# Retention heads of a decoder step: the samples' states weighted by q on ScalarE and VectorE, and the last block of scores in three fp32r passes

## Chip, cores and metric

One core of one Trainium2 chip runs the whole program. The metric is the device time of one execution in microseconds; the kernel before takes 2317.14 us in the median of 3 runs (2315.48 to 2318.4).

## The reference, cut to what matters

One layer of a hybrid decoder works on 256 prompt rows and 8 sample rows at once. The part that the change touches is retention: 8 heads, 256 channels of q and k, 512 of v per head. For the prompt, in chunks of 128 rows:

```python
scores = jnp.einsum('bhld,bhmd->bhlm', q, k) * decay[None]
q_dec = q * jnp.exp((idx[None, :] + 1.0) * log_g[:, None])[None, :, :, None]
o = jnp.einsum('bhlm,bhmv->bhlv', scores, v) + jnp.einsum('bhld,bhdv->bhlv', q_dec, S)
k_dec = k * jnp.exp((L - 1.0 - idx[None, :]) * log_g[:, None])[None, :, :, None]
S_new = jnp.exp(L * log_g)[None, :, None, None] * S + jnp.einsum('bhmd,bhmv->bhdv', k_dec, v)
```

For each of the 8 samples there is one new row and a state S of 256 x 512 per head, read from memory: S becomes g S + k v, is written back, and the output row is q S (512 numbers per sample and head). Then follow a group norm over each head's 512 channels, a gate, and projections. All of it is fp32.

## The kernel before, in words

Activations stand transposed: channels on the 128 partitions, 264 columns (256 prompt rows, 8 samples). Every large product is a stream over weight chunks of 512 x 256 (`gemm`, `project`): SyncE loads a chunk, ScalarE rounds it to fp32r (`wh_...`, line 199), VectorE takes the remainder (`wl_...`, line 200), and TensorE makes 24 matmuls of 128x128 by 264 columns, three fp32r passes for each tile (`gemm_part`, lines 213 to 215). Three buffers each hold `wh` and `wl`, six the raw chunks.

The stretch around the change is the loop over the 8 heads. While head h does its retention, TensorE works on the input projections of head h + 1 (`acc_in`), on the output projection of head h - 1 (`acc_pa`) and on the modulation (`mp`, with 32-column weights in four column groups of the array). `spread` lays the 18 steps of `retention` between these chunks, and a scheduler in the framework then sets the order on each engine; engines take their instructions strictly in that order, so the order is fixed before the run.

The steps of one head that matter:

- `sample_rows`, `scores`, `values`, `keys` prepare: the samples' v rows (`vsr`), the decayed scores, the transposed v blocks in two halves m = 0 and 1 (`vh`, `vl`), k times its decay.
- `sample(b)`, eight times: GpSimd's queue loads the state tile `S` (128 x 2 x 512), VectorE copies v's row b to all partitions (`vb`, line 620), ScalarE multiplies `S` by the head's g (line 621), VectorE adds k v in two instructions (line 623), GpSimd's queue stores `S`.
- `sample_q(half)`, twice: q S on TensorE. For four samples and both halves d of the 256 channels there is a matmul of 32 weight columns (`z`, a q column set among zeros, copied by GpSimd at line 546) and 512 moving columns (line 634), each sample in its own column group, all into one tile `qp`. `S` has to stay until then.
- `sample_out`: `qp` holds the eight rows spread over the column groups; four fp32 matmuls with a 0/1 matrix of 8 columns (line 644, `osp`) gather and transpose them into `o`.
- `prompt_out(i)`: for each of the four blocks of 128 v channels, three fp32r matmuls over 256 columns for m = 0 (lines 597 to 599) and one plain fp32 matmul over 128 columns for m = 1 (line 600, from `vt` and `sct`).
- `prompt_state`, `centre`, `gate` (line 610 is the last product of `prompt_state`) end the head; their `yh`, `yl` feed `project` of the next head.

Of the kernel before, what the change touches and what calls it, by code (L numbers as in the profile page):

```python
# [20 lines left out]
F32 = mybir.dt.float32  # L21
F32R = mybir.dt.float32r
AF = mybir.ActivationFunctionType
ALU = mybir.AluOpType
# [27 lines left out]
C_SELQ = C_SELM + 9  # L52
C_KD = C_SELQ + 8
# [7 lines left out]
def constants():  # L61
# [7 lines left out]
    for j in range(4):  # L69
        for i in range(9):  # L70
            c[32 * j + i, C_SELM + i] = 1.0
        c[32 * j + j, C_SELQ + j] = 1.0
        c[32 * j + 4 + j, C_SELQ + 4 + j] = 1.0
# [59 lines left out]
def build(ctx, tc, a):  # L133
# [365 lines left out]
    qz = []  # L499
    for i in range(2):  # L500
        z = hp.tile([P, 2, 2, 32], F32, tag=f"qz{i}", name=f"qz{i}")
        ve.memset(z, 0.0)
        qz.append(z)
# [25 lines left out]
    def retention(h):  # L529

        q, k, v, gr = raw_q[h], raw_k[h], raw_v[h], raw_gr[h]
        z = qz[h % 2]
        st = {}

        def sample_rows():
# [8 lines left out]
            for half in range(2):  # L544
                c = slice(4 * half, 4 * half + 4)
                gp.tensor_copy(out=z[:, half, :, c], in_=q[:, :, TP + 4 * half:TP + 4 * half + 4])

        def scores():
# [8 lines left out]
            st["sct"] = hp.tile([P, 384], F32, tag="sct", name=f"sct{h}")  # L557
            ve.tensor_tensor(out=st["sct"], in0=scp[:, :384], in1=dec, op=ALU.mult)
            st["scs"] = [hp.tile([P, 256], F32R, tag=f"sc{n}", name=f"sc{n}{h}") for n in ("hi", "lo")]
            split_act(st["sct"][:, 0:256], *st["scs"])  # L560

        def values(m):
# [6 lines left out]
            if m:  # L569
                st["vt"] = hp.tile([P, DV], F32, tag="vt", name=f"vt{h}")  # L570
                sc.copy(out=st["vt"], in_=vtp)
            split_act(st["vt"] if m else vtp, vh, vl)
# [15 lines left out]
        def prompt_out(i):  # L588
# [3 lines left out]
            (vh, vl), (sh, sl) = st["vs", 0], st["scs"]  # L592
            for j in range(2):
                vi = 2 * i + j
                c = slice(vi * P, (vi + 1) * P)
                out = op[:, j * 256:j * 256 + 256]
                te.matmul(out=out, lhsT=vh[:, c], rhs=sh, start=True, stop=False)
                te.matmul(out=out, lhsT=vh[:, c], rhs=sl, start=False, stop=False)
                te.matmul(out=out, lhsT=vl[:, c], rhs=sh, start=False, stop=False)
                te.matmul(out=out[:, P:], lhsT=st["vt"][:, c], rhs=st["sct"][:, 256:384], start=False, stop=True)  # L600
# [14 lines left out]
        def sample(b):  # L615

            s = hp.tile([P, 2, DV], F32, tag="S", name=f"S{h}_{b}", bufs=5)
# [8 lines left out]
            st["S", b] = s  # L626

        def sample_q(half):
# [3 lines left out]
            for d in range(2):  # L632
                for j in range(4):
# [334 lines left out]
```

## Time and profile before

| | |
|---|---|
| median of 3 runs | 2317.14 us (2315.48 to 2318.4) |
| the profiled execution's own time | 2321.42 us |
| its span, first to last instruction | 2319.7 us |
| PE busy in the span | 2288.5 us (99%) |
| VectorE (DVE) busy | 1457.3 us (63%) |
| ScalarE (ACT) busy | 1054.6 us (45%) |
| GpSimd (POOL) busy | 233.7 us (10%) |
| granted TensorE clock, mean | 0.997 |

The profile records each instruction of one execution with its start and its duration. Matmuls overlap in the array: one of 264 columns is recorded with 0.28 us, but the next starts 0.12 us later. So what a matmul costs is read here from start to start, not from its duration. A plain fp32 matmul is recorded as two instructions, an fp32r matmul or a transpose as one. PEld are the weight loads, which run beside the matmuls.

### The profile page before, as it was taken

What the parts mean: (1) busy time and instruction counts of PE and PEld (TensorE: products, weight loads), DVE (VectorE), ACT (ScalarE), POOL (GpSimd) and SP (SyncE); (2) the same over time, 40 slices, a digit from 0 to 9 for tenths busy, and PEclk for the clock granted to TensorE, in tenths of its full rate; (3) what the DMA queues carried; (4) which work ended last, traced back from release to release, by engine and by line L of the source; (5) the groups of instructions that cost most, each with busy time, mean ns of one, the idle gap of its engine ahead of it and who ended that gap; (6) DMA issues with size and microseconds to landing.
All of it is one profiled execution on the core that took longest, in us unless ns stands there. A gap on an engine that the chain in (4) does not pass through costs nothing. (4 is left out here: it accounts for less than half of the span.)

```text
span 2319.7 us, 44798 instructions
## 1 busy us (share of the span) xinstructions
PE 2288.5 (99%) x18496; PEld 2141.6 (92%) x18496; DVE 1457.3 (63%) x2078; ACT 1054.6 (45%) x1306; POOL 233.7 (10%) x404
## 2 busy tenths in 40 slices
PE   8999999999999999999999999999999999999997
PEld 6899998898998989898989999989999999999997
DVE  4676675676666666666665567576666666654444
ACT  4333354345454444454435454454444444444342
POOL 0000132021112020102010101111000000000000
PEclk9999999999999999999999999999999999999998
DMA  9788877897779696869687879856666665565663
GB/s 325 243 264 274 263 211 260 300 345 284 263 270 326 201 326 198 293 221 326 200 282 229 277 244 324 323 170 192 207 201 196 201 213 183 182 192 185 189 190 104
DMA packets 171581, 561.14 MB, mean 242 GB/s; under 512 B 18448, under 2 KB 32848, under 8 KB 171376
## 3 DMA queue, kind: packets, MB, share of 16 engines
q1 hardware_dynamic: 147376, 474.08, 62.8%
q0 software_dynamic: 23568, 83.73, 10.0%
q8 instruction: 145, 2.38, 0.4%
q10 hardware_dynamic: 432, 0.47, 0.1%
q14 instruction: 60, 0.49, 0.1%
HBM read 509.82 MB, written 48.38 MB: 241 GB/s over the span
## 5 line engine op out<-in xcount | busy, mean ns | idle before, releaser
L213 PE MATMUL acc_up<-h_hi,wh_up 128*128 128x264 f32 x1408 | 400.9, 285 | 1.6 <-ACT h_hi L204 1.6
L214 PE MATMUL acc_up<-h_lo,wh_up 128*128 128x264 f32 x1408 | 400.2, 284 | 0.6 <-DVE h_lo L205 0.6
L215 PE MATMUL acc_up<-h_hi,wl_up 128*128 128x264 f32 x1408 | 399.5, 284 | 0.0
L213 PE MATMUL acc_in<-h_hi,wh_in 128*128 128x264 f32 x1344 | 388.3, 289 | 0.0
L214 PE MATMUL acc_in<-h_lo,wh_in 128*128 128x264 f32 x1344 | 382.6, 285 | 0.0
L215 PE MATMUL acc_in<-h_hi,wl_in 128*128 128x264 f32 x1344 | 381.6, 284 | 0.0
L200 DVE TENSOR_TENSOR wl_up<-w_up,wh_up 128x1024 fp32r<-128x1024 f32 x176 | 215.9, 1227 | 179.7 <-ACT wh_up L199 179.5
L200 DVE TENSOR_TENSOR wl_in<-w_in,wh_in 128x1024 fp32r<-128x1024 f32 x168 | 205.0, 1222 | 158.3 <-ACT wh_in L199 142.4
L199 ACT CAST wh_in<-w_in 128x1024 fp32r<-128x1024 f32 x168 | 175.9, 1048 | 272.6 <-PE acc_in L214 162.3
L199 ACT CAST wh_up<-w_up 128x1024 fp32r<-128x1024 f32 x176 | 184.6, 1049 | 250.0 <-issue 142.8
L213 PEld LDWEIGHTS acc_up<-h_hi,wh_up 128*128 128x128 f32 x1408 | 265.4, 189 | 8.3 <-issue 5.9
L213 PEld LDWEIGHTS acc_in<-h_hi,wh_in 128*128 128x128 f32 x1344 | 252.9, 188 | 19.8 <-issue 14.3
L214 PEld LDWEIGHTS acc_up<-h_lo,wh_up 128*128 128x128 f32 x1408 | 265.7, 189 | 0.8 <-DVE h_lo L205 0.8
L215 PEld LDWEIGHTS acc_up<-h_hi,wl_up 128*128 128x128 f32 x1408 | 265.1, 188 | 0.0
L215 PEld LDWEIGHTS acc_in<-h_hi,wl_in 128*128 128x128 f32 x1344 | 252.5, 188 | 6.1 <-issue 5.0
L214 PEld LDWEIGHTS acc_in<-h_lo,wh_in 128*128 128x128 f32 x1344 | 253.0, 188 | 1.3 <-issue 0.8
L213 PE MATMUL acc_st<-h_hi,wh_st 128*128 128x264 f32 x704 | 203.7, 290 | 0.3 <-ACT ue L402 0.3
L215 PE MATMUL acc_st<-h_hi,wl_st 128*128 128x264 f32 x704 | 200.5, 286 | 2.2 <-DVE wl_st L200 2.2
L214 PE MATMUL acc_st<-h_lo,wh_st 128*128 128x264 f32 x704 | 199.9, 284 | 0.0
L214 PE MATMUL acc_dn<-f_lo,wh_dn 128*128 128x264 f32 x704 | 199.7, 284 | 0.0
L215 PE MATMUL acc_dn<-f_hi,wl_dn 128*128 128x264 f32 x704 | 199.6, 284 | 0.0
L213 PE MATMUL acc_dn<-f_hi,wh_dn 128*128 128x264 f32 x704 | 199.6, 284 | 0.0
(257 smaller groups left out, 5254.1 us busy)
## 6 DMA issues: line engine op xcount, KB each, us to landing
wm<-in_w_mod SPq DMA_DIRECT2D x176, 512.0 KB, 5.1
w_up<-in_w_up SPq DMA_DIRECT2D x176, 512.0 KB, 4.3
w_in<-in_w_in SPq DMA_DIRECT2D x168, 512.0 KB, 5.2
w_dn<-in_w_down SPq DMA_DIRECT2D x88, 512.0 KB, 3.7
S<-in_state_ret POOLq DMA_DIRECT2D x64, 512.0 KB, 7.8
out_rs<-S POOLq DMA_DIRECT2D x64, 512.0 KB, 5.0
w_pa<-in_w_proj_a SPq DMA_DIRECT2D x64, 512.0 KB, 4.4
w_st<-in_w_in SPq DMA_DIRECT2D x66, 384.0 KB, 4.2
```

Of the source, the lines that this page charges most:

```text
L199: sc.copy(out=hi, in_=w)
L200: ve.tensor_tensor(out=lo, in0=w, in1=hi.bitcast(F32), op=ALU.subtract)
L213: te.matmul(out=acc[:, b, :T], lhsT=hi[:, k, cols], rhs=xh[:, k0 + k, :], start=s, stop=False)
L214: te.matmul(out=acc[:, b, :T], lhsT=hi[:, k, cols], rhs=xl[:, k0 + k, :], start=False, stop=False)
L215: te.matmul(out=acc[:, b, :T], lhsT=lo[:, k, cols], rhs=xh[:, k0 + k, :], start=False, stop=e)
```

## The change

`sample(b)` now goes on after the update of `S`: ScalarE multiplies the first half of the state by q's column (`qt`, 128 x 512), and VectorE multiplies the second half by q's other column and adds it to `qt`. `S` is free after that and the store, and its buffers go from 5 to 4; `qt` has 4. `sample_q(half)` then has only to add up the 128 partitions: one matmul per sample with `pick`, whose 32 columns are ones in column 0 (first half) or 1 (second half) and zeros elsewhere. `sample_out` takes four transposes in place of the four selection matmuls, and VectorE's copy picks the eight rows out. The GpSimd copies into `z` are gone.

For m = 1 of `prompt_out` the plain fp32 matmul becomes three fp32r passes over 128 columns. The scores of all 384 columns are rounded and split, in place of 256, the copy `vt` is gone, and `dec` is overwritten in place of a tile `sct`.

```diff
@@ -49,8 +49,7 @@
 
 C_ID = 0
 C_SELM = C_ID + P
-C_SELQ = C_SELM + 9
-C_KD = C_SELQ + 8
+C_KD = C_SELM + 9
 C_CNT = C_KD + 16
 C_N = C_CNT + 64
 
@@ -69,8 +68,6 @@
     for j in range(4):
         for i in range(9):
             c[32 * j + i, C_SELM + i] = 1.0
-        c[32 * j + j, C_SELQ + j] = 1.0
-        c[32 * j + 4 + j, C_SELQ + 4 + j] = 1.0
     g = 1.0 - 2.0 ** (-5.0 - np.arange(H, dtype=np.float64))
     m = np.arange(TP, dtype=np.float64)
     for h in range(H):
@@ -496,11 +493,11 @@
     psum_phase("heads", True)
     rot = hp.tile([P, 2 * T], F32, tag="rot", name="rot")
     gp.dma_start(out=rot, in_=a["rot"])
-    qz = []
+
+    pick = hp.tile([P, 2, 32], F32, tag="pick", name="pick")
+    ve.memset(pick, 0.0)
     for i in range(2):
-        z = hp.tile([P, 2, 2, 32], F32, tag=f"qz{i}", name=f"qz{i}")
-        ve.memset(z, 0.0)
-        qz.append(z)
+        ve.memset(pick[:, i, i:i + 1], 1.0)
 
     def rotate(x0, x1, dst, scale, name):
         cos, sin = rot[:, 0:T], rot[:, T:2 * T]
@@ -529,7 +526,6 @@
     def retention(h):
 
         q, k, v, gr = raw_q[h], raw_k[h], raw_v[h], raw_gr[h]
-        z = qz[h % 2]
         st = {}
 
         def sample_rows():
@@ -541,9 +537,6 @@
                 te.transpose(vsp[:, i * P:(i + 1) * P], vsc[:, i].rearrange("p r b -> p (r b)"), ident)
             st["vsr"] = hp.tile([P, DV], F32, tag="vsr", name=f"vsr{h}")
             sc.copy(out=st["vsr"], in_=vsp)
-            for half in range(2):
-                c = slice(4 * half, 4 * half + 4)
-                gp.tensor_copy(out=z[:, half, :, c], in_=q[:, :, TP + 4 * half:TP + 4 * half + 4])
 
         def scores():
 
@@ -554,10 +547,9 @@
                 for d in range(2):
                     te.matmul(out=scp[:, c0:c0 + n], lhsT=k[:, d, m0:m0 + P], rhs=q[:, d, l0:l0 + n],
                               start=d == 0, stop=d == 1)
-            st["sct"] = hp.tile([P, 384], F32, tag="sct", name=f"sct{h}")
-            ve.tensor_tensor(out=st["sct"], in0=scp[:, :384], in1=dec, op=ALU.mult)
-            st["scs"] = [hp.tile([P, 256], F32R, tag=f"sc{n}", name=f"sc{n}{h}") for n in ("hi", "lo")]
-            split_act(st["sct"][:, 0:256], *st["scs"])
+            ve.tensor_tensor(out=dec, in0=scp[:, :384], in1=dec, op=ALU.mult)
+            st["scs"] = [hp.tile([P, 384], F32R, tag=f"sc{n}", name=f"sc{n}{h}") for n in ("hi", "lo")]
+            split_act(dec, *st["scs"])
 
         def values(m):
 
@@ -566,10 +558,7 @@
                 te.transpose(vtp[:, i * P:(i + 1) * P], v[:, i, m * P:(m + 1) * P], ident)
             vh = hp.tile([P, DV], F32R, tag=f"vh{m}", name=f"vh{h}_{m}")
             vl = hp.tile([P, DV], F32R, tag=f"vl{m}", name=f"vl{h}_{m}")
-            if m:
-                st["vt"] = hp.tile([P, DV], F32, tag="vt", name=f"vt{h}")
-                sc.copy(out=st["vt"], in_=vtp)
-            split_act(st["vt"] if m else vtp, vh, vl)
+            split_act(vtp, vh, vl)
             st["vs", m] = vh, vl
 
         def keys():
@@ -589,15 +578,16 @@
             if i == 0:
                 st["o"] = hp.tile([P, 4, T], F32, tag="o", name=f"o{h}")
             op = psx(f"op{h}_{i}")
-            (vh, vl), (sh, sl) = st["vs", 0], st["scs"]
+            sh, sl = st["scs"]
             for j in range(2):
                 vi = 2 * i + j
                 c = slice(vi * P, (vi + 1) * P)
-                out = op[:, j * 256:j * 256 + 256]
-                te.matmul(out=out, lhsT=vh[:, c], rhs=sh, start=True, stop=False)
-                te.matmul(out=out, lhsT=vh[:, c], rhs=sl, start=False, stop=False)
-                te.matmul(out=out, lhsT=vl[:, c], rhs=sh, start=False, stop=False)
-                te.matmul(out=out[:, P:], lhsT=st["vt"][:, c], rhs=st["sct"][:, 256:384], start=False, stop=True)
+                for m, (out, l) in enumerate(((op[:, j * 256:j * 256 + 256], slice(0, 256)),
+                                              (op[:, j * 256 + P:j * 256 + 256], slice(256, 384)))):
+                    vh, vl = st["vs", m]
+                    te.matmul(out=out, lhsT=vh[:, c], rhs=sh[:, l], start=m == 0, stop=False)
+                    te.matmul(out=out, lhsT=vh[:, c], rhs=sl[:, l], start=False, stop=False)
+                    te.matmul(out=out, lhsT=vl[:, c], rhs=sh[:, l], start=False, stop=m == 1)
             sc.copy(out=st["o"][:, 2 * i:2 * i + 2, 0:TP], in_=op.rearrange("p (j t) -> p j t", j=2))
 
         def prompt_state(d):
@@ -614,7 +604,7 @@
 
         def sample(b):
 
-            s = hp.tile([P, 2, DV], F32, tag="S", name=f"S{h}_{b}", bufs=5)
+            s = hp.tile([P, 2, DV], F32, tag="S", name=f"S{h}_{b}", bufs=4)
             gp.dma_start(out=s, in_=a["state_ret"][b, h].rearrange("(d p) v -> p d v", p=P))
             vb = hp.tile([P, DV], F32, tag="vb", name=f"vb{h}_{b}", bufs=2)
             ve.stream_shuffle(out=vb, in_=st["vsr"], mask=[b] * 32)
@@ -623,17 +613,20 @@
                 ve.scalar_tensor_tensor(out=s[:, d, :], in0=vb, scalar=k[:, d, TP + b:TP + b + 1],
                                         in1=s[:, d, :], op0=ALU.mult, op1=ALU.add)
             gp.dma_start(out=a["rs"][b, h].rearrange("(d p) v -> p d v", p=P), in_=s)
-            st["S", b] = s
+
+            t = hp.tile([P, DV], F32, tag="qt", name=f"qt{h}_{b}", bufs=4)
+            sc.mul(out=t, in_=s[:, 0, :], mul=q[:, 0, TP + b:TP + b + 1])
+            ve.scalar_tensor_tensor(out=t, in0=s[:, 1, :], scalar=q[:, 1, TP + b:TP + b + 1], in1=t,
+                                    op0=ALU.mult, op1=ALU.add)
+            st["qt", b] = t
 
         def sample_q(half):
 
             if half == 0:
                 st["qp"] = psx(f"qp{h}")
-            for d in range(2):
-                for j in range(4):
-                    te.matmul(out=st["qp"][32 * j:32 * j + 32, :], lhsT=z[:, half, d, :],
-                              rhs=st["S", 4 * half + j][:, d, :], start=half + d == 0, stop=half + d == 2,
-                              tile_position=(0, 32 * j))
+            for j in range(4):
+                te.matmul(out=st["qp"][32 * j:32 * j + 32, :], lhsT=pick[:, half, :], rhs=st["qt", 4 * half + j],
+                          start=half == 0, stop=half == 1, tile_position=(0, 32 * j))
             if half:
                 st["qs"] = hp.tile([P, DV], F32, tag="ev", name=f"qs{h}")
                 sc.copy(out=st["qs"], in_=st["qp"])
@@ -641,9 +634,9 @@
         def sample_out():
             osp = psx(f"osp{h}")
             for i in range(4):
-                te.matmul(out=osp[:, i * NS:(i + 1) * NS], lhsT=st["qs"][:, i * P:(i + 1) * P],
-                          rhs=cst[:, C_SELQ:C_SELQ + NS], start=True, stop=True)
-            ve.tensor_copy(out=st["o"][:, :, TP:T], in_=osp[:, 0:4 * NS].rearrange("p (i b) -> p i b", i=4))
+                te.transpose(osp[:, i * P:(i + 1) * P], st["qs"][:, i * P:(i + 1) * P], ident)
+            ve.tensor_copy(out=st["o"][:, :, TP:T].rearrange("p i (m j) -> p i m j", m=2),
+                           in_=osp.rearrange("p (i j r) -> p i r j", i=4, j=4)[:, :, 0:2, :])
 
         def head_sum(src, name):
             s2 = hp.tile([P, 2, T], F32, tag="s2", name=f"s2_{name}_{h}")
@@ -699,7 +692,7 @@
 
     def gate_a(g):
         def use(_, acc):
-            s = hp.tile([P, 2, DV], F32, tag="S", name=f"sga{g}", bufs=5)[:, :, :T]
+            s = hp.tile([P, 2, DV], F32, tag="S", name=f"sga{g}", bufs=4)[:, :, :T]
             sc.activation(out=s, in_=acc[:, :, :T], func=AF.Sigmoid)
             sy.dma_start(out=dram["sga"][:, 2 * g:2 * g + 2, :], in_=s)
 
@@ -726,9 +719,9 @@
     m_lo = acts.tile([P, KT, T], F32R, tag="a_lo", name="m_lo")
     for g in range(8):
         k = slice(2 * g, 2 * g + 2)
-        sga = hp.tile([P, 2, DV], F32, tag="S", name=f"sgr{g}", bufs=5)[:, :, :T]
+        sga = hp.tile([P, 2, DV], F32, tag="S", name=f"sgr{g}", bufs=4)[:, :, :T]
         sy.dma_start(out=sga, in_=dram["sga"][:, k, :])
-        yb = hp.tile([P, 2, DV], F32, tag="S", name=f"ybr{g}", bufs=5)[:, :, :T]
+        yb = hp.tile([P, 2, DV], F32, tag="S", name=f"ybr{g}", bufs=4)[:, :, :T]
         sy.dma_start(out=yb, in_=dram["yb"][:, k, :])
         project(H - 1, g)
         t = y_a[:, k, :]
```

The scheduler's order changes with it. First, TensorE in head 3, second half of the samples. Names are out<-moving,weights with the framework's numbers; `mp` is the modulation, `qp` the sample products, `acc_pa` the output projection. Before:

```order
L214 MATMUL acc_pa_4_9587<-yl_8928,wh_pa_4_9590 128x264
L634 MATMUL qp_9792<-S_3_9520,qz_5424 32x512
L634 MATMUL qp_9792<-S_4_9651,qz_5424 32x512
L634 MATMUL qp_9792<-S_5_9723,qz_5424 32x512
L634 MATMUL qp_9792<-S_6_9862,qz_5424 32x512
L634 MATMUL qp_9792<-S_7_9909,qz_5424 32x512
L634 MATMUL qp_9792<-S_4_9651,qz_5424 32x512
L634 MATMUL qp_9792<-S_5_9723,qz_5424 32x512
L634 MATMUL qp_9792<-S_6_9862,qz_5424 32x512
L634 MATMUL qp_9792<-S_7_9909,qz_5424 32x512
L215 MATMUL acc_pa_4_9587<-yh_8927,wl_pa_4_9591 128x264
```

Now, where the second half of the same head begins:

```order
L211 MATMUL acc_in_9487<-h_lo,wh_in_2_9561 128x264
L628 MATMUL qp_9870<-qt_4_9731,pick 32x512
L628 MATMUL qp_9870<-qt_5_9806,pick 32x512
L210 MATMUL acc_pa_4_9659<-yh_8984,wh_pa_4_9662 128x264
L211 MATMUL acc_pa_4_9659<-yl_8985,wh_pa_4_9662 128x264
L212 MATMUL acc_in_9487<-h_hi,wl_in_2_9562 128x264
```

The nine products in one run have become four, one for each sample, and they no longer stand together: samples 4 and 5 are here, samples 6 and 7 stand alone, 28 and 51 rows further on, each between two matmuls of `acc_in` or `acc_pa`.

Second, TensorE in the same head, one block of `prompt_out`. `sct` are the scores of the last 128 columns in fp32, `schi`, `sclo` the split ones. Before:

```order
L597 MATMUL op_0_9369<-schi_9083,vh_0_9153 128x256
L598 MATMUL op_0_9369<-sclo_9084,vh_0_9153 128x256
L599 MATMUL op_0_9369<-schi_9083,vl_0_9154 128x256
L600 MATMUL op_0_9369<-sct_9081,vt_9164 128x128
```

Now:

```order
L588 MATMUL op_0_9427<-schi_9137,vh_0_9207 128x256
L589 MATMUL op_0_9427<-sclo_9138,vh_0_9207 128x256
L590 MATMUL op_0_9427<-schi_9137,vl_0_9208 128x256
L588 MATMUL op_0_9427<-schi_9137,vh_1_9216 128x128
L589 MATMUL op_0_9427<-sclo_9138,vh_1_9216 128x128
L590 MATMUL op_0_9427<-schi_9137,vl_1_9217 128x128
```

One matmul on `sct` and `vt` has become three on split scores and the split v of m = 1 (`vh_1`, `vl_1`).

Third, ScalarE in the same head, around the last samples. `wh_in` and `wh_pa` are roundings of weight chunks, `S` the multiplication by g, `so` a copy of the prompt's state. Before:

```order
L621 ACTIVATE S_5_9723<-S_5_9723 128x1024
L199 CAST wh_in_3_9530<-w_in_3_9528 128x1024
L621 ACTIVATE S_6_9862<-S_6_9862 128x1024
L621 ACTIVATE S_7_9909<-S_7_9909 128x1024
L199 CAST wh_pa_4_9590<-w_pa_4_9588 128x1024
L199 CAST wh_pa_5_9622<-w_pa_5_9620 128x1024
L199 CAST wh_pa_6_9662<-w_pa_6_9660 128x1024
```

Now:

```order
L611 ACTIVATE S_7_9986<-S_7_9986 128x1024
L618 ACTIVATE qt_4_9731<-S_4_9723,q_7721 128x512
L618 ACTIVATE qt_5_9806<-S_5_9798,q_7721 128x512
L196 CAST wh_in_2_9561<-w_in_2_9559 128x1024
L618 ACTIVATE qt_6_9944<-S_6_9936,q_7721 128x512
L196 CAST wh_in_3_9602<-w_in_3_9600 128x1024
L602 COPY so_1_9656<-sp_1_9649 128x512
L618 ACTIVATE qt_7_9994<-S_7_9986,q_7721 128x512
L196 CAST wh_pa_4_9662<-w_pa_4_9660 128x1024
L611 ACTIVATE S_0_10576<-S_0_10576 128x1024
L196 CAST wh_pa_5_9694<-w_pa_5_9692 128x1024
```

Four multiplications into `qt` have come among the roundings. Each reads a state that VectorE must have finished, and ScalarE takes the rounding behind it only afterwards.

## Rows read from the trace of the kernel before

**Rows 1.** The page, part 1: busy time and share of the span of each engine.

```profile
PE 2288.5 (99%) x18496; PEld 2141.6 (92%) x18496; DVE 1457.3 (63%) x2078; ACT 1054.6 (45%) x1306; POOL 233.7 (10%) x404
```

**Rows 2.** Waits of PE over the whole span: who waited for whom, total us, times, longest.

```profile
PE acc_ga L215 <- DVE wl_ga L200: 1.1, 1, 1.1
```

**Rows 3.** Busy time by engine in the heads' stretch, then granted clock, DMA share, GB/s.

```profile
470.00:1370.00 900.00, 898.86 (x7035) 814.68 (x7035) 583.16 (x806) 430.90 (x491) 116.95 (x169) 1.00 0.79 268
```

**Rows 4.** PE timeline, end of head 0: start us, duration us, instruction, merged count.

```profile
549.38 0.28 PE L213 MATMUL acc_in<-h_hi,wh_in 128*128 128x264 f32 x1
549.59 1.06 PE L634 MATMUL qp<-S,qz 128*32 128x512 f32 x8
550.58 0.39 PE L214 MATMUL acc_in<-h_lo,wh_in 128*128 128x264 f32 x1
550.90 1.04 PE L634 MATMUL qp<-S,qz 128*32 128x512 f32 x2
551.88 0.39 PE L215 MATMUL acc_in<-h_hi,wl_in 128*128 128x264 f32 x1
552.10 0.29 PE L213 MATMUL acc_in<-h_hi,wh_in 128*128 128x264 f32 x1
```

**Rows 5.** PE timeline, head 3, the long run of sample products.

```profile
850.96 0.28 PE L214 MATMUL acc_pa<-yl,wh_pa 128*128 128x264 f32 x1
851.17 2.76 PE L634 MATMUL qp<-S,qz 128*32 128x512 f32 x18
853.86 0.39 PE L215 MATMUL acc_pa<-yh,wl_pa 128*128 128x264 f32 x1
854.09 0.29 PE L213 MATMUL acc_pa<-yh,wh_pa 128*128 128x264 f32 x1
```

**Rows 6.** PE timeline, head 2, half of the selection matmuls of the sample outputs.

```profile
744.42 0.29 PE L215 MATMUL acc_pa<-yh,wl_pa 128*128 128x264 f32 x1
744.54 0.51 PE L644 MATMUL osp<-cst,qs 128*128 128x8 f32 x4
744.91 0.37 PE L213 MATMUL acc_pa<-yh,wh_pa 128*128 128x264 f32 x1
745.11 0.28 PE L214 MATMUL acc_pa<-yl,wh_pa 128*128 128x264 f32 x1
```

**Rows 7.** PE timeline, head 3, four transposes.

```profile
800.04 0.28 PE L213 MATMUL acc_in<-h_hi,wh_in 128*128 128x264 f32 x1
800.16 0.60 PE L541 MATMUL vsp<-cst,vsc 128*128 128x128 f32 x4
800.52 0.37 PE L214 MATMUL acc_in<-h_lo,wh_in 128*128 128x264 f32 x1
800.73 0.28 PE L215 MATMUL acc_in<-h_hi,wl_in 128*128 128x264 f32 x1
```

**Rows 8.** PE timeline, head 7, one column block of the prompt output.

```profile
1290.47 0.38 PE L600 MATMUL op<-sct,vt 128*128 128x128 f32 x2
1290.93 0.28 PE L599 MATMUL op<-schi,vl 128*128 128x256 f32 x1
1291.04 0.38 PE L600 MATMUL op<-sct,vt 128*128 128x128 f32 x2
```

**Rows 9.** Tiles op and osp, weight loads (fp32r, fp32): duration ns min/median/max.

```profile
L599 PEld LDWEIGHTS op<-schi,vl x32: 187/188/192, 505.4 to 1291.4; 128*128 128x128 f32 x32
L644 PEld LDWEIGHTS osp<-cst,qs x64: 187/192/193, 554.9 to 1357.8; 128*128 128x128 f32 x64
```

**Rows 10.** Groups by line on DVE and ACT, the heads' stretch: busy us, mean ns.

```profile
L623 DVE SCALAR_TENSOR_TENSOR S<-vb,k,S 128x512 f32<-128x512 f32 x128 | 89.5, 744 | 25.6 <-ACT S L621 25.5
L571 ACT COPY vt<-vtp 128x512 f32<-128x512 f32 x8 | 4.7, 590 | 0.0
```

**Rows 11.** Waits of DVE and of ACT, the heads' stretch.

```profile
DVE y_a L698 <- PE acc_pa L215: 70.6, 33, 4.8
ACT S L621 <- DMA S<-in_state_ret: 25.3, 18, 8.4
```

## Prediction

> **What bounds the kernel now.** I read the engines' busy times first: TensorE is busy in 99% of the span, VectorE in 63%, ScalarE in 45% [rows 1]. Then TensorE's waits: in the loop over the heads the list has hardly one, the longest being 1.1 us for a remainder from VectorE [rows 2]. Then the stretch that the change touches, 470 to 1370 us: TensorE is busy for 898.86 of 900 us at a granted clock of 1.00, that is 2.4 GHz; VectorE has 317 us free, ScalarE 469 [rows 3]. So in this stretch the time is the sum of what TensorE's instructions cost, from start to start, and an instruction saved there is time saved, as long as the other two still deliver their weights in time. What remains is to price TensorE's instructions, and for that I read its timeline. The unit: a matmul of the big products starts 0.12 us after the one ahead (744.42 to 744.54) [rows 6].
>
> **The sample products: fewer rounds, more runs.** From 549.38 to 552.10 TensorE does three ordinary matmuls and two runs of sample products, one of four matmuls (eight records), one of a single matmul (two records) [rows 4]. 2.72 us less 3 x 0.12 leaves 2.36, or 1.18 us a run. A run of one therefore costs about what a run of four does: the four column groups work side by side, and one round of them is the unit. The run of nine matmuls needs three rounds, since a column group comes up to three times; it takes 854.09 - 850.96 - 2 x 0.12 = 2.89 us [rows 5]. So a further round costs (2.89 - 1.18) / 2 = 0.86, and entering and leaving a run 1.18 - 0.86 = 0.32.
>
> The new order halves the sample matmuls, from 128 to 64, but splits them: 25 runs with 44 rounds become 30 runs with 30. Some stand beside matmuls of the modulation (`mp`), which run in the same column groups, so I count both kinds together in the order lists, for all runs of 512 columns in the program: 91 runs with 119 rounds before, 90 with 103 now. That is 1 x 0.32 + 16 x 0.86 = **14.1 us less**. Halving the matmuls of unbroken runs would have given 22 x 0.86 = 18.9 or more; the splitting takes the rest.
>
> **The sample outputs.** Half of a head's selection matmuls (four records) cost 745.11 - 744.42 - 2 x 0.12 = 0.45 us, so a head's eight 0.90 [rows 6]. Four transposes of 128x128 cost 800.73 - 800.04 - 0.24 = 0.45 [rows 7]. They take the place of the eight records: 8 x 0.45 = **3.6 us less**. VectorE's copy of 8 x 4 numbers stays and only reads farther apart.
>
> **The last scores.** A column block goes from 1290.47 to 1291.04: one plain fp32 matmul of 128 columns and three fp32r matmuls of 256, which start 0.11 to 0.12 apart [rows 8]. 0.57 - 3 x 0.12 leaves 0.21 for the fp32 one; 32 of them are 6.7 us. In their place come 96 fp32r matmuls of 128 columns, and the trace has no fp32r matmul that short. Below, the price goes with the columns: 0.12 x 128 / 264 = 0.06. Above, it is that of the whole fp32 matmul, 0.21. I take 0.11, because the selection matmuls have 8 columns, almost nothing to stream, and still cost 0.45 / 4 = 0.11 each [rows 6]: each brings new 128x128 weights, and the fp32r matmul brings new ones too, with a load recorded at the same length, 187 to 192 ns [rows 9]. 96 x 0.112 = 10.8, so **4.1 us more**, between 1.1 less and 13.5 more.
>
> The Trainium skill, page "TensorE: Matmul & The Clock Gate", section "Back-to-back issue gap", gives about 81 ns for each matmul in a stream of weight loads and matmuls of 128 columns. By it the term would be 96 x 0.081 = 7.8, 1.1 us more in place of 4.1, and the whole 2301; no row of the kernel before shows such a stream in fp32r.
>
> **The start stage.** The scheduler also regroups the modulation's runs of 256 columns in the first stage: one run and one round more, 0.32 + 0.86 / 2 = **0.8 us more**.
>
> **What is hidden.** VectorE gets 64 instructions like that on `S`, 744 ns each [rows 10]: 47.6 us, so 631 us in a stretch of some 890. ScalarE gets 64 of 128 x 512 and loses eight copies of that size at 590 ns [rows 10]: 33 us more, 464. The wider split of the scores adds half of its 256 columns once per head on both. All this lies beside TensorE's matmuls; the cover is the three buffers of split weights, that is up to two chunks, 2 x 24 x 0.12 = 5.8 us, of work that TensorE has ahead. GpSimd loses 16 copies. The state tiles lose a buffer, but no longer wait for the product: their next load waits for VectorE and the store, as the store did before. I put all this at 0, with bounds of 1 us less (the wait in [rows 2] came from a late state) and 23 us more (third rival).
>
> **Sum.** -14.1 - 3.6 + 4.1 + 0.8 = -12.8 us. Against the profiled execution's 2321.4 us that is 2308.6; the median of the runs lies 4.3 us below that execution, so the forecast for a median is 2317.1 - 12.8 = **2304 us**.
>
> **Rivals.**
>
> *Short fp32r matmuls are cheap.* If their price goes with the columns, 0.06 each, the last term is -1.1 and the sum -18.0: 2299 us. For it: at 264 and 256 columns the pace fits the columns as well as the load. Against it: the 8-column matmuls at 0.11. The page's 81 ns lies between this and my value.
>
> *Short fp32r matmuls cost as fp32 ones.* At 0.21 each the term is +13.5 and the sum -3.4: 2314 us, which a measurement can hardly tell from no change (some 0.2%, 4.6 us). Nothing in the trace speaks for it but that no such matmul is there.
>
> *Late roundings: slower.* The place is ScalarE's queue behind the multiplications into `qt` of samples 4 to 7. Each waits until VectorE has finished the state, 2 x 0.74 = 1.5 us of work [rows 10], and VectorE's queue has the additions into `y_a` between, which wait for TensorE up to 4.8 us [rows 11]. Behind the multiplication stands the rounding of the weights that TensorE needs next. A wait of 4.8, the 1.5, and four multiplications of 0.59 hold ScalarE for 8.7 us; 5.8 are covered, 2.9 are not. Once in each head that is 23 us, sum +10.4: 2327 us. It decides from 12.8 / 8 = 1.6 us a head on. For it: order and waits are there. Against it: ScalarE waited 25.3 us for late states in the kernel before, once for 8.4 us [rows 11], and of all that 1.1 us reached TensorE [rows 2]; and a VectorE that waits for TensorE means that TensorE still has work.
>
> *A little of that.* Half a microsecond a head lost: -8.8, 2308 us.
>
> That the change does not do what it says is no rival: the order list has 64 products, 32 transposes and 96 short passes.
>
> **How the numbers follow.** Forecast 0.55, cheap passes 0.15, a little waiting 0.10, dear passes 0.12, late roundings 0.08. The first three are faster by over 0.2%, and of the fourth, which lies just inside that bound, a small part: 0.83 faster, 0.11 same, 0.06 slower. The range reaches from just below the cheap passes to the dear ones, 2298 to 2314; outside it lie the late roundings and some little on either side.
>
> **What would show it.** In the changed kernel's timeline a run of one to four sample products should still cost 1.18 us; four transposes 0.45; three short passes 0.34 from start to start (0.18 or 0.63 by the first two rivals). TensorE's waits should stay near 1 us in the heads' stretch; a new wait of `acc_pa` or `acc_in` for `wh_...` on ScalarE would be the third rival. The forecast is wrong if TensorE's instructions cost what I say and the time still doesn't fall, or if the short passes differ from 0.11.

## The result, and the profile after

The changed kernel takes **2305.14 us** in the median of four runs (2302.22 to 2305.84), the kernel before 2317.53 (2315.48 to 2318.40). The ratio is 0.9941, with a 95% interval of 0.9929 to 0.9952: 12.4 us, or 0.5% of the median, faster. The forecast was 2304.

Part 1 of the page of the changed kernel, which answers to [rows 1]:

```profile
PE 2273.3 (99%) x18368; PEld 2135.7 (93%) x18368; DVE 1501.6 (65%) x2143; ACT 1090.5 (47%) x1362; POOL 221.7 (10%) x388
```

The heads' stretch by engine, which answers to [rows 3], and the PE waits of that stretch:

```profile
470.00:1370.00 900.00, 898.70 (x7022) 824.23 (x7021) 633.76 (x879) 475.05 (x556) 107.04 (x153) 1.00 0.79 272
```

```profile
PE sp L598 <- ACT o L591: 1.2, 5, 0.4
```

VectorE went from 583 to 634 busy us and ScalarE from 431 to 475, and TensorE still has work in all but 1.3 us of 900. The one wait that the list gives for the stretch is new and small: the state products (`sp`, line 598) wait for ScalarE's copy of the prompt outputs into `o`.

The PE timeline of the changed kernel, at four places: a run of one sample product, a run of four, the four transposes of a head, and a column block of the prompt output. The columns are start us, duration us, instruction, merged count.

```profile
729.71 0.28 PE L211 MATMUL acc_in<-h_lo,wh_in 128*128 128x264 f32 x1
729.93 1.04 PE L628 MATMUL qp<-qt,pick 128*32 128x512 f32 x2
730.90 0.39 PE L212 MATMUL acc_in<-h_hi,wl_in 128*128 128x264 f32 x1
731.13 0.29 PE L210 MATMUL acc_in<-h_hi,wh_in 128*128 128x264 f32 x1
...
545.98 0.28 PE L212 MATMUL acc_in<-h_hi,wl_in 128*128 128x264 f32 x1
546.19 1.06 PE L628 MATMUL qp<-qt,pick 128*32 128x512 f32 x8
547.19 0.39 PE L210 MATMUL acc_in<-h_hi,wh_in 128*128 128x264 f32 x1
547.41 0.28 PE L211 MATMUL acc_in<-h_lo,wh_in 128*128 128x264 f32 x1
...
659.66 0.28 PE L212 MATMUL acc_in<-h_hi,wl_in 128*128 128x264 f32 x1
659.78 0.60 PE L637 MATMUL osp<-cst,qs 128*128 128x128 f32 x4
660.13 0.37 PE L210 MATMUL acc_in<-h_hi,wh_in 128*128 128x264 f32 x1
660.34 0.28 PE L211 MATMUL acc_in<-h_lo,wh_in 128*128 128x264 f32 x1
...
590.85 0.33 PE L588 MATMUL op<-schi,vh 128*128 128x256 f32 x1
591.01 0.28 PE L589 MATMUL op<-sclo,vh 128*128 128x256 f32 x1
591.13 0.28 PE L590 MATMUL op<-schi,vl 128*128 128x256 f32 x1
591.25 0.23 PE L588 MATMUL op<-schi,vh 128*128 128x128 f32 x1
591.32 0.27 PE L589 MATMUL op<-sclo,vh 128*128 128x128 f32 x1
591.42 0.27 PE L590 MATMUL op<-schi,vl 128*128 128x128 f32 x1
591.53 0.33 PE L588 MATMUL op<-schi,vh 128*128 128x256 f32 x1
```

Read each from the matmul ahead to the second one behind, less 0.12 for each of the two big matmuls. The run of one: 731.13 - 729.71 - 0.24 = 1.18 us. The run of four: 547.41 - 545.98 - 0.24 = 1.19. The transposes: 0.44. A block of three wide and three short passes: 591.53 - 590.85 = 0.68, less 3 x 0.12 leaves 0.32, or 0.11 for a short pass.

The same reading over all of TensorE's records, from the first `acc_in` of the heads' stretch to the last `acc_pa`, puts all that isn't a big product in groups (sums of start to start, worked out from the records of both traces). Where different kinds stand in one run, the time at their edges can be shared out in more than one way, which moves the sums of a group by up to some 3 us and the changes by some 0.5:

| us | before | after | change | forecast |
|---|---|---|---|---|
| runs in column groups (`mp`, `qp`) | 95.1 | 80.4 | -14.7 | -14.1 |
| sample outputs (`osp`) | 7.2 | 3.6 | -3.6 | -3.6 |
| prompt outputs, state products, `ktp` beside them | 42.2 | 48.4 | +6.2 | +4.1 |
| all else | 31.2 | 30.9 | -0.3 | 0 |
| the rest: gaps between big products | | | -1.4 | 0 (-1 to +23) |
| the whole stretch | 946.1 | 932.35 | -13.75 | |

The first stage grew by 0.2 (forecast 0.8). After the heads the profiled execution of the changed kernel is another 2.0 us shorter, though nothing there was changed; 1.5 of them lie in the `acc_up` stage and 0.5 behind the `acc_dn` stage. The first 6 us of the `acc_up` stage tell of the 1.5 (columns as in [rows 3]), first before, then after:

```profile
1521.00:1524.00 3.00, 1.59 (x7) 1.38 (x8) 3.00 (x10) 1.95 (x6) 0.00 (x0) 0.79 0.81 287
1524.00:1527.00 3.00, 3.00 (x18) 3.00 (x18) 3.00 (x9) 1.62 (x4) 0.00 (x0) 0.64 0.16 63
```

```profile
1508.00:1511.00 3.00, 2.18 (x16) 1.98 (x17) 3.00 (x9) 1.63 (x5) 0.00 (x0) 1.00 0.90 330
1511.00:1514.00 3.00, 3.00 (x27) 3.00 (x26) 3.00 (x9) 2.01 (x4) 0.00 (x0) 1.00 0.02 7
```

The granted clock was 0.79 and 0.64 before, which are means over 3 us of time at 1.2 and at 2.4 GHz, and 1.00 after; `acc_up` took 522.77 and 521.31 us. So 1.5 of the 15.6 us between the two spans are this, which is no gain of the change. The medians differ by 12.4 and not by 15.6, as the profiled execution of the kernel before lies 4 us above its median. Of the ten kernels below, seven show the longer `acc_up` stage in their profiled execution and three the shorter.

### The profile page after: what moved, and what is told of

Read it like the earlier page. It is cut to its first block, busy times and chain, and to the rows that moved or that the text cites. A ratio compares the mean times of both kernels' runs of the same rounds, so it can differ in the third digit from the quotient of the medians.

```text
span 2304.1 us, 44683 instructions
## 1 busy us (share of the span) xinstructions
PE 2273.3 (99%) x18368; PEld 2135.7 (93%) x18368; DVE 1501.6 (65%) x2143; ACT 1090.5 (47%) x1362; POOL 221.7 (10%) x388
## 4 chain that ended last, share of the span: by engine, by line
PE 91%; DMA 3%; DVE 3%; issue 1%; ACT 1%; POOL 0%; DVEq 0%; SPq 0%; POOLq 0%; ACTq 0%
PE acc_up L210 7%; PE acc_up L211 7%; PE acc_up L212 7%; PE acc_in L210 7%; PE acc_in L212 7%; PE acc_in L211 7%; PE acc_dn L211 4%; PE acc_dn L210 4%; PE acc_dn L212 4%; PE acc_st L210 4%; PE acc_st L212 3%; PE acc_st L211 3%; PE mp L283 3%; PE acc_pa L210 2%; PE acc_pa L212 2%; PE acc_pa L211 2%
## 5 line engine op out<-in xcount | busy, mean ns | idle before, releaser
L210 PEld LDWEIGHTS acc_in<-h_hi,wh_in 128*128 128x128 f32 x1344 | 252.9, 188 | 15.6 <-issue 10.9
L212 PEld LDWEIGHTS acc_in<-h_hi,wl_in 128*128 128x128 f32 x1344 | 252.5, 188 | 10.2 <-DVE q L508 4.2
```

The lines of the kernel that those rows point to most:

```text
L210: te.matmul(out=acc[:, b, :T], lhsT=hi[:, k, cols], rhs=xh[:, k0 + k, :], start=s, stop=False)
L212: te.matmul(out=acc[:, b, :T], lhsT=lo[:, k, cols], rhs=xh[:, k0 + k, :], start=False, stop=e)
```

## The experiments

The theory: in the heads' stretch the time is the sum of TensorE's start-to-start prices over its written order. A run in column groups costs 0.32 us plus 0.86 a round, whatever it fills; a 128-column fp32r pass 0.11 to 0.12; what ScalarE and VectorE do besides is covered. The main rival: the gain came from the number of sample products, 128 to 64, and the order doesn't matter.

**1. The four products of a half held together.** Nothing is left out or added on TensorE; the column of ones is made to depend on the fourth product of states and q:

```diff
+pk = hp.tile([P, 32], F32, tag=f"pk{half}", name=f"pk{h}_{half}")
+ve.scalar_tensor_tensor(out=pk, in0=st["qt", 4 * half + 3][:, 0:32], scalar=0.0, in1=pick[:, half, :],
+                        op0=ALU.mult, op1=ALU.add)
-te.matmul(out=st["qp"][32 * j:32 * j + 32, :], lhsT=pick[:, half, :], rhs=st["qt", 4 * half + j],
+te.matmul(out=st["qp"][32 * j:32 * j + 32, :], lhsT=pk, rhs=st["qt", 4 * half + j],
```

> The changed kernel with the four sample products of a half made to come due together (the column of ones that all four read now depends on the last of the four products of states and q; the arithmetic is the same). Written order: the runs of 512-column matmuls in column groups go from 90 with 103 rounds to 83 with 93; the sample products alone from 30 runs to 18. Theory A (a run costs 0.32 us to enter and leave and 0.86 us per round, however many of the four column groups it fills): 7 x 0.32 + 10 x 0.86 = 10.9 us less, 2305.1 - 10.9 = 2294 us. Rival B (the saving of the change was the number of sample products, 128 to 64, each at some 0.22 us): their number is the same as in the changed kernel, so 2305 us. Rival C (the products held back make the PE wait for the last of the four): up to 16 halves x 1.3 us, the ACT and DVE pair of one sample, added to A's figure, 2294 to 2315 us, and waits of sample products for qt appear among the PE's waits.

Measured: 2299.09 us (2295.20 to 2300.31); against before 0.9913 [0.9897, 0.9929]. The column-group runs fell from 80.4 to 69.5 us, 10.9 as theory A has it, with as many products as before: rival B falls. Against the changed kernel's 2305.14 only 6.0 came out. In the profiled execution 4.3 us went to one place, where the scores of head 0 waited for k. First the PE wait, then the 3 us in which it ends (columns as in [rows 3]):

```profile
PE scp L548 <- DVE k L507: 2.6, 1, 2.6
```

```profile
494.00:497.00 3.00, 1.99 (x5) 1.63 (x6) 3.00 (x7) 3.00 (x5) 0.00 (x0) 0.58 0.47 143
```

The wait itself is 2.6 us. Behind it the granted clock was 0.58, that is for most of these 3 us at 1.2 GHz, and the scores and transposes there took 1.7 us longer than the same ones in the changed kernel. No sample product waited for `qt`, so rival C falls; this wait is another one. The rotation of k stood behind a remainder of `wl_in` on VectorE, whose weight chunk came late.

**2. The last scores in fp32 again.** The changed kernel with the one fp32 matmul restored (`vt` kept, in the buffer that `so` and `qs` use):

```diff
-for m, (out, l) in enumerate(((op[:, j * 256:j * 256 + 256], slice(0, 256)),
-                              (op[:, j * 256 + P:j * 256 + 256], slice(256, 384)))):
...
+te.matmul(out=out[:, P:], lhsT=st["vt"][:, c], rhs=st["sct"][:, 256:384], start=False, stop=True)
```

> The changed kernel with the last 128 columns of the scores as one fp32 matmul again (32 of them in place of 96 fp32r passes). Theory A (a 128-column fp32r pass costs 0.117 us from start to start, a fp32 matmul of 128 columns 0.21): 96 x 0.117 - 32 x 0.21 = 4.5 us less; the written order has 94 runs with 104 rounds of column-group matmuls in place of 90 with 103, 4 x 0.32 + 0.86 = 2.1 us more; together -2.4, 2302.7 us. Rival B (the short passes cost half of a 256-column pass, the rest of what the trace puts on them is noise of the records): 96 x 0.06 - 32 x 0.21 = -1.0, so 1.0 us more by the passes and 2.1 by the order, 2308 us.

Measured: 2309.63 us (2307.65 to 2312.62); 0.9963 [0.9949, 0.9977]. Both theories miss on the time. The matmuls themselves cost what A says: in head 1, eight fp32 records and ten wide passes take 2.07 us, which leaves 0.22 for a fp32 matmul (two records). But the state products that follow came to stand idle. PE timeline, then ACT timeline of this kernel, head 2:

```profile
707.57 0.39 PE L593 MATMUL op<-dec,vt 128*128 128x128 f32 x2
708.32 0.50 PE L601 MATMUL sp<-vh,kh 128*128 128x512 f32 x1 [0.36 <-ACT o L594]
```

```profile
706.74 1.06 ACT L614 ACTIVATE S<-S 128x1024 f32<-128x1024 f32 x1 [0.23 <-DMA S<-in_state_ret]
707.70 0.57 ACT L594 COPY o<-op 128x512 f32<-128x512 f32 x1
```

The copy that frees the accumulator stands behind a state's decay on ScalarE; a shorter group on TensorE only reaches that wait sooner. Its total over the run is 2.7 us where it was 1.2. Against the changed kernel, the stretch grew by 2.7 us. By the records, the outputs and state products lost 3.0 us of work, where A had 4.5, and gained 1.8 of waits; the runs in column groups grew by 3.2, where A had 2.1, since the changed kernel executes 102 rounds and not the 103 that were counted (experiment 7 shows why); the gaps between big products grew by 0.8. 1.5 more is the clock after the heads.

**3. The same, with the copies of the outputs on VectorE.**

```diff
-sc.copy(out=st["o"][:, 2 * i:2 * i + 2, 0:TP], in_=op.rearrange("p (j t) -> p j t", j=2))
+ve.tensor_copy(out=st["o"][:, 2 * i:2 * i + 2, 0:TP], in_=op.rearrange("p (j t) -> p j t", j=2))
```

> The kernel with fp32 last scores (2309.6 us), with the two copies of the prompt outputs into o per head on DVE in place of ACT. Written order: 91 runs with 105 rounds where that kernel has 94 with 104, 0.1 us less. Theory A (what the fp32 scores gained was given back because the state products waited for the copy of the outputs in ACT's queue, behind the decay of a sample's state): the PE's waits of sp for o, 2.7 us there, go to near 0, and the time to 2307 us. Rival (the copy is late for another reason, or DVE's queue is no shorter): the wait stays at 2 to 3 us or moves to another line, 2309 to 2310 us.

Measured: 2309.07 us (2308.03 to 2312.73); 0.9964 [0.9950, 0.9978]. The wait of `sp` for `o` is gone from the list, as A expected, but the time is not: the rival was right that it moves, and A's reason for the loss in experiment 2 is at most a part of it. The largest wait of the stretch is now

```profile
PE mp L283 <- DMA wm<-in_w_mod: 3.6, 3, 1.8
```

**4. Both, held together and fp32 scores.** The diffs of 1 and 2.

> The products held together (as in the run before) and the last scores in fp32 at once. The written order has 83 runs with 93 rounds, as with the products held together alone. Theory A: -10.9 (runs) - 4.5 (scores) = -15.4, 2289.7 us, the fastest of all. Rival B (number of products and column price): 2305 + 1 = 2306 us.

Measured: 2297.48 us (2293.35 to 2301.41); 0.9910 [0.9894, 0.9925]. Rival B falls again; of A's 15.4 us only 7.7 arrived. The lowest run is within 4 us of A. Where some of it went, in the PE and the ACT timeline of this kernel:

```profile
1070.62 1.06 PE L634 MATMUL qp<-qt,pk 128*32 128x512 f32 x8
1073.54 0.39 PE L210 MATMUL acc_pa<-yh,wh_pa 128*128 128x264 f32 x1 [1.85 <-ACT v L518]
```

```profile
1071.00 1.06 ACT L614 ACTIVATE S<-S 128x1024 f32<-128x1024 f32 x1 [5.08 <-DMA S<-in_state_ret]
1072.89 0.59 ACT L518 COPY v<-acc_in 128x528 f32<-128x528 f32 x1
```

ScalarE waits 5.08 us for a state tile, and the copy of v, which TensorE needs, is queued behind it. The waits that TensorE's list gives for the heads' stretch come to 6.2 us here (3.2 for v, 2.7 of `sp` for `o`, 0.3 for `wl_in`), where they were 1.2 in the changed kernel: that is 5.0 of the 7.7 that didn't arrive.

**5. Both, with the copies on VectorE.** The diffs of 1, 2 and 3.

> The kernel with products held together and fp32 last scores (2297.5 us), with the same copies on DVE. Written order: 82 runs with 91 rounds in place of 83 with 93, 2.0 us less. Theory A: 2.0 less by the order and up to 2.7 less by the waits of sp for o: 2293 us. Rival (the waits for late states on ACT that this kernel shows, 3.2 us of acc_pa behind the copy of v, don't depend on the copies, and DVE's copies delay its remainders of weights): 2296 to 2299 us, with waits of acc_ for wl tiles.

Measured: 2298.52 us (2293.13 to 2300.85); 0.9913 [0.9899, 0.9926]. No gain over experiment 4. In the profiled execution `mp` waits 4.7 us for its weights' DMA in the heads' stretch; VectorE's remainders are not late to speak of (`wl_in` 0.7), so the rival had the time and not the reason.

**6. Each short pass cut in two.**

```diff
-                              (op[:, j * 256 + P:j * 256 + 256], slice(256, 384)))):
-    vh, vl = st["vs", m]
+                              (op[:, j * 256 + P:j * 256 + P + 64], slice(256, 320)),
+                              (op[:, j * 256 + P + 64:j * 256 + 256], slice(320, 384)))):
+    vh, vl = st["vs", min(m, 1)]
```

> The changed kernel with each of the 96 short fp32r passes cut into two of 64 columns, 192 in all; the same columns in sum. The written order has 89 runs with 101 rounds of column-group matmuls in place of 90 with 103, 2.0 us less. Theory A (a short pass costs what its weight load and issue cost, 0.117 us, whatever its columns): 96 x 0.117 = 11.2 more, less 2.0, 2314.3 us, and a group of 12 full and 24 cut passes takes 36 x 0.117 = 4.2 us. Rival B (the price goes by columns): nothing more, 2303 us. Rival C (64 columns have a lower floor than 128, say half way): 2308 to 2309 us.

Measured: 2315.36 us (2312.95 to 2317.59); 0.9987 [0.9978, 0.9995], 10.2 more than the changed kernel. PE timeline, six passes of 64 columns in head 7:

```profile
1284.49 0.36 PE L589 MATMUL op<-schi,vh 128*128 128x256 f32 x1
...
1284.81 0.28 PE L591 MATMUL op<-schi,vl 128*128 128x256 f32 x1
1284.93 0.19 PE L589 MATMUL op<-schi,vh 128*128 128x64 f32 x1
...
1285.40 0.28 PE L591 MATMUL op<-schi,vl 128*128 128x64 f32 x1
1285.51 0.36 PE L589 MATMUL op<-schi,vh 128*128 128x256 f32 x1
```

From the first wide pass of one block to that of the next, 1284.49 to 1285.51, are 1.02 us; less 3 x 0.12, six passes take 0.66 or 0.11 each. Over the whole stretch the outputs and state products took 10.1 us more of work, 0.105 for each of the 96 added passes. The runs in column groups took 1.2 less (89 with 101 rounds where the changed kernel executes 90 with 102), and waits and gaps 0.8 less: the heads' stretch grew by 8.0. The longer `acc_up` stage adds 1.5. 64 columns cost as much as 128, and those nearly as much as 256: in this range the price is by the matmul, not by the column. Each of these matmuls comes with its own weight load, so that the runs don't show which of the two sets it. Rivals B and C fall. Above 256 columns the column counts again: the state products, fp32r passes of 512 columns, start 0.23 us apart in the changed kernel:

```profile
599.67 0.39 PE L599 MATMUL sp<-vl,kh 128*128 128x512 f32 x1
599.90 0.39 PE L598 MATMUL sp<-vh,kh 128*128 128x512 f32 x1
```

**7. The scores alone, on the kernel before.** The change's lines on the scores, the split of the values and the short passes, and nothing else:

```diff
-te.matmul(out=out[:, P:], lhsT=st["vt"][:, c], rhs=st["sct"][:, 256:384], start=False, stop=True)
+for m, (out, l) in enumerate(((op[:, j * 256:j * 256 + 256], slice(0, 256)),
+                              (op[:, j * 256 + P:j * 256 + 256], slice(256, 384)))):
...
```

> The kernel before with one part of the change alone: the last scores in three fp32r passes. Written order: 101 runs with 126 rounds of column-group matmuls where the kernel before has 91 with 119, though no such matmul was touched. Theory A (start-to-start prices and the written order): 10 x 0.32 + 7 x 0.86 = 9.2 more by the order and 96 x 0.117 - 32 x 0.21 = 4.5 by the passes, 2317.5 + 13.7 = 2331 us; some 2 us less if the longer group covers the copy of the outputs by ACT that the state products wait for (that wait was 1.2 us in the changed kernel and 2.7 us with fp32 scores): 2329 us. Rival (the parts of a change add, each with its own price): 2322 us.

Measured: 2326.16 us (2324.11 to 2326.46); 1.0032 [1.0020, 1.0044]. The time lies between the two. A's count of rounds was too high at five places; four of them look like this one (PE timeline):

```profile
751.69 0.28 PE L215 MATMUL acc_pa<-yh,wl_pa 128*128 128x264 f32 x1
751.90 0.62 PE L286 MATMUL mp<-wm,csil 128*32 128x512 f32 x2
751.91 0.62 PE L631 MATMUL qp<-S,qz 128*32 128x512 f32 x1
...
752.89 0.39 PE L213 MATMUL acc_in<-h_hi,wh_in 128*128 128x264 f32 x1
753.12 0.28 PE L214 MATMUL acc_in<-h_lo,wh_in 128*128 128x264 f32 x1
```

Two matmuls of the modulation and a sample product share this run, for 753.12 - 751.69 - 0.24 = 1.19 us: by their places in the order they fall in different column groups, so it is one round where I had counted two. Counted by column group, this kernel has 121 rounds and the kernel before 119, so the order costs 10 x 0.32 + 2 x 0.86 = 4.9 us; the records give 5.0. The outputs and state products grew by 3.6, where the passes were priced at 4.5. The rest nearly cancels: the scores waited 1.7 us for k, the wait of 1.1 in [rows 2] is gone and the other gaps are shorter. Together the stretch grew by 8.3. The 2 us of cover in A's lower figure have nothing to stand on: neither this kernel nor the kernel before has a wait of `sp` for `o` in its list. All this was worked out after the result.

**8. The transposes alone, on the kernel before.**

```diff
-te.matmul(out=osp[:, i * NS:(i + 1) * NS], lhsT=st["qs"][:, i * P:(i + 1) * P],
-          rhs=cst[:, C_SELQ:C_SELQ + NS], start=True, stop=True)
+te.transpose(osp[:, i * P:(i + 1) * P], st["qs"][:, i * P:(i + 1) * P], ident)
```

> The kernel before with one part of the change alone: the samples' rows come back by four transposes, and two strided copies pick the eight columns. Written order: 94 runs with 122 rounds of column-group matmuls in place of 91 with 119. Theory A: 8 heads x (0.90 - 0.45) = 3.6 less by the transposes, 3 x 0.32 + 3 x 0.86 = 3.5 more by the order, 2317.4 us, no change; the transposes themselves show 0.45 us per head. Rival (the parts add): 2313.9 us.

Measured: 2319.47 us (2314.50 to 2324.61); 1.0005 [0.9995, 1.0015], no difference. The sample outputs' matmuls fell from 7.19 to 3.57 us as priced, the column-group runs grew from 95.1 to 98.6: the part's gain is there and the scheduler's new order spends it. The parts of this change don't add; the rival falls.

**9 and 10. The side work done twice**, once on the changed kernel and once on that of experiment 1:

```diff
+sc.mul(out=vb, in_=s[:, 0, :], mul=q[:, 0, TP + b:TP + b + 1])
+ve.scalar_tensor_tensor(out=vb, in0=s[:, 1, :], scalar=q[:, 1, TP + b:TP + b + 1], in1=vb,
+                        op0=ALU.mult, op1=ALU.add)
 st["qt", b] = t
```

> The changed kernel with the products of states and q made twice, the second time into a buffer that nobody reads after: 64 ACT multiplications of 0.59 to 0.7 us and 64 DVE operations of 0.74 us more. Written order: 106 runs with 122 rounds in place of 90 with 103. Theory A (the side work is covered by the PE, only the order counts): 16 x 0.32 + 19 x 0.86 = 21.5 more, 2326.6 us. Rival B (the side work costs nothing and neither does the order): 2305 us. Rival C (the side work isn't covered any more): on top of A's figure up to 48 us of DVE, 2330 to 2374 us, and waits of the PE for qt or wl tiles grow by that much.

> The same doubled products of states and q, put on the kernel in which the four sample products of a half come due together. Written order: 82 runs with 96 rounds where that kernel has 83 with 93. Theory A: 3 x 0.86 - 0.32 = 2.3 more than that kernel's 2299, 2301 us, although ACT and DVE do the same extra work as in the run before: the two differ by some 25 us through the order alone. Rival C (the side work isn't covered): 2310 us or more, with waits of the PE for qt, pk or wl tiles.

Measured: 2325.07 us (2323.95 to 2329.32), 1.0030 [1.0019, 1.0041], and 2298.61 us (2295.17 to 2299.96), 0.9912 [0.9900, 0.9925]. The same extra work stands in both; 26 us lie between them. In the heads' stretch of the first one TensorE waited for nothing that the list shows, and its busy time is 900.00 of 900 us. Its runs in column groups took 20.5 us more than those of the changed kernel, of 19.9 in the time: it loses by its order. The second one's stretch, with the busiest VectorE and ScalarE of all:

```profile
470.00:1370.00 900.00, 899.02 (x7096) 832.70 (x7096) 680.91 (x965) 519.46 (x624) 106.51 (x153) 1.00 0.80 274
```

681 and 519 us of side work in 900, and TensorE still has 899. So the cover was never near its end at 634 and 475, and rival C falls in both.

## Why the prediction was right, step by step

**TensorE bounds the stretch.** Right. Busy 898.70 of 900 us after [rows 3], and doubling the added work on the other engines cost nothing where the order nearly stayed (experiment 10).

**A run of one costs as a run of four; 1.18 a run, 0.86 a further round.** Right: 1.18 and 1.19 in the rows above, against [rows 4, 5]. The sum over all runs was -14.7 where the forecast had -14.1, and experiment 1 moved it by another -10.9 with the number of products fixed. So runs that are less broken save 25.6 us against the kernel before, where the prediction gave 18.9 or more, and 10.9 of that the changed kernel leaves unused. The Trainium skill, page "TensorEngine Tiling (Array Packing)", section "Key Properties", says that a change of tiling mode drains TensorE; the 0.32 us for entering and leaving agree with it, though no run shows how much of the 0.32 is that drain. One detail was wrong: I had added the rounds of modulation and sample products in a run, and they share a round where their column groups differ. Experiment 7 showed it, but the changed kernel has such a run too: from 614.41 to 615.84 two matmuls of the modulation and a sample product take 1.19 us. So its count is 102 rounds and not 103, 0.86 us less than the prediction says, which is about the 0.6 by which the forecast of this term was short.

**The transposes, 0.45 a head for 0.90.** Right: 0.44 and 3.6 us in all [rows 6, 7].

**The short passes at 0.112.** Right: 0.11, and still 0.11 at 64 columns, so the cheap and the dear rival both fall. By the Trainium skill's 81 ns (page "TensorE: Matmul & The Clock Gate", section "Back-to-back issue gap") they would have been cheaper; in this kernel the rows show 0.11, and the measurement decides. The reason given was that each pass brings new weights; the runs show that columns hardly matter from 64 to 256, not that the weight load sets the 0.11.

**What was priced at 0.** Nearly right, and partly by luck. The group of outputs and state products grew by 6.2, not 4.1: 1.2 us of it are waits for ScalarE's copy into `o`, a wait that the prediction didn't name; the other 0.9 isn't traced to a cause. It was paid for by the waits that went: 1.4 us in the gaps between big products, with the `wl_ga` wait of [rows 2] among them, in which a late state had stood. So +2.1 here, -0.6 in the runs, -1.4 in the gaps and -0.3 elsewhere cancel, and the sum came out closer than its terms. ScalarE's load was 475 us, not 464: a multiplication into `qt` takes 0.72 us and not the 0.59 of the copies. That changed no time, as the load was covered.

**The third rival, late roundings.** Its wait came, but small. Three waits in the heads' stretch of the changed kernel bear on it: ScalarE for states from memory, ScalarE's multiplications into `qt` for the states that VectorE finishes, and VectorE's additions into `y_a` for TensorE.

```profile
ACT S L611 <- DMA S<-in_state_ret: 21.8, 16, 3.7
...
ACT qt L618 <- DVE S L613: 6.9, 7, 1.3
```

```profile
DVE y_a L691 <- PE acc_pa L212: 26.2, 24, 3.0
```

The wait for `qt` is 6.9 us in seven of 64 multiplications, where the rival had 6.3 us of waiting in each head, and TensorE's list has no wait for a `wh_`. The other two are less than before [rows 11]. The engine was right, though, if not the cause: in experiment 4 the copy of v in ScalarE's queue, behind a state that DMA brought late, held TensorE up for 3.2 us in three waits, the longest 1.85.

What stays open: why experiments 1, 4, 5 and 10 all end at 2297 to 2299 us, with runs spread over 5 to 8 us. Their profiled executions show different waits (k, v, `wm`); those that were followed stand behind loads that came late, and whether one queue is behind them was not tried. That the state tiles have a buffer less was not tried by itself either; with it ScalarE waited less for states than before, 21.8 us for 25.3. Nor is it settled what makes the clock fall at 1521 us in some executions: TensorE was idle for about 2 us around it in both executions (1.41 of the first 3 us before, 0.82 after, and 0.69 and 1.28 in the 4 us ahead of them).

## What to carry to other kernels

Where TensorE is full, price an edit from start to start in the timeline, count runs and rounds in the written order, and count them anew for every variant: here an edit that touched no matmul in column groups lost 3.5 us through the order, and one dependency that kept four matmuls together gained 6. Three narrow passes are no cheaper than three wide ones: a pass costs 0.11 us here at 64 and 128 columns and 0.12 at 256 (and 0.23 at 512). And when such a kernel gets faster, expect part of the gain to go into waits that TensorE's work had covered: of 10.9 us 6.0 arrived, of 15.4 only 7.7. Such a wait can cost more than its length: 2.6 us in experiment 1 became 4.3, as the granted clock was low behind it.

## What was not expected of the hardware

A fp32r pass of 64 columns starts 0.11 us after the one ahead, as one of 128 does. A sample product and two modulation matmuls, which write different tiles and belong to different accumulations, ran in one round of 1.19 us; where, by their places in the order, their column groups met, the run took 2.04 (experiment 9, from the matmul ahead to the one behind):

```profile
721.22 0.28 PE L212 MATMUL acc_pa<-yh,wl_pa 128*128 128x264 f32 x1
721.43 1.05 PE L283 MATMUL mp<-wm,csil 128*32 128x512 f32 x4
722.32 1.02 PE L631 MATMUL qp<-qt,pick 128*32 128x512 f32 x2
723.27 0.39 PE L210 MATMUL acc_in<-h_hi,wh_in 128*128 128x264 f32 x1
723.50 0.29 PE L211 MATMUL acc_in<-h_lo,wh_in 128*128 128x264 f32 x1
```

The column group of a matmul isn't in the trace; it is taken here from the kernel's loops, which go through the four in turn. So counted, a run has as many rounds as its fullest group has matmuls, and this fits the time of every run of both kinds in the kernel before, the changed one and experiments 7 to 10.

The granted clock at the start of one stage, 0.64 to 0.79 or 1.00, moves the span by 1.5 us between executions whose work there is the same.
